# Attention loads in a written order: the next row tile's query stacks ahead of the latent keys and queries

## The chip, the cores and the metric

One core of one Trainium2 chip runs the whole program. The metric is device time in microseconds (us); three runs of the kernel before gave 1340.05, 1340.75 and 1341.09 us, median 1340.75.

## What is computed

A trunk of two equal layers on x of 1024 rows and 1024 columns, all in float32. A layer projects the normalised rows once, splits the columns among three attention groups, multiplies each group's output by a SiLU gate, and projects back. Cut to that:

```python
h = rms_norm(x, g_norm)
z = h @ w_in                      # 2656 columns, split among A, B, C and gates
oa = dense_gqa(qa, ka, va) * silu(ag)          # A: 6 heads, 2 key heads, all 1024 keys
ob = windowed_sink_gqa(qb, kb, vb) * silu(bg)  # B: 6 heads, 2 key heads, |i-j| <= 128
oc = mla(qc, kc, vc) * silu(cg)                # C: 4 heads from low-rank latents, all keys
x = x + concat(oa, ob, oc) @ w_out
```

A final RMSNorm closes the trunk.

## The kernel before

Each operand of a product is held as a high and a low part (`hi` rounded, `lo` the rest), so that a float32 product is two or three matmuls. Rows stand in 8 row tiles of 128 (`NS`).

A layer has these stages. The input projection makes rotated queries and keys of A and B (`pza`, `pzb`), the latents of C (`pzc`) and writes them to device memory: `d_q` (queries), `d_k` (keys of A and B), `d_kn` and `d_k3` (latent keys of C), `d_vc` (its values). Then `gate_units` computes the gates: 12 units here called g_m_hf (m the gate column block, hf the half of the rows), each 24 matmuls `pg`, one SiLU on ACT (L617) into a tile `g` that has two buffers, and one DMA of 256 KB to `d_gate`, issued by ACT itself. The last six, in this order, are g_3_0, g_4_0, g_5_0, g_3_1, g_4_1, g_5_1.

Then comes attention. Its loads are all issued by SyncE's queue (SP) through the helper `dma` (L97). First the tiles of the first row tile: `qsta` and `qstb` (query stacks of A and B, four DMAs of 96 KB each), `ka0`, `ka1` (high and low keys of A, two halves of 512 KB each), `kb0`, `kb1` (the same for B), a mask. Then latent values `vC` (1 MB), gates `gta`, `gtb`, `gtc`, latent keys `k1`, `k2`, `k3` (six DMAs, 2.25 MB), the latent queries `qc` of three row tiles (five DMAs each, 256 KB a tile), and the query stacks of the next row tile. The generator `units()` yields units of work: `UnitA` (scores `sa` of one A head, exp, transposes `ppa`, values `poa`), `UnitB` (scores `sb` of three B heads), `UnitC` (scores `sc`). For each row tile qt it makes two `Gqa` objects, whose constructor issues the stack loads; units of C come in from the second row tile on (`C_AT`).

The order of instructions on an engine isn't that of the code: a scheduler picks it, by priorities and a timeline of its own, except for instructions that `tc.keep_in_program_order` pins. What it picks is then fixed in the program.

Every DMA that SP or ACT issues also counts on one of eight completion counters, DMAHW0 to DMAHW7, called lanes below. SP's and ACT's DMAs take the lanes in turn, in the order in which the scheduler laid them down, and one that takes a lane is issued only when the lane's holder before it has landed. Waiting DMAs hold up all that stand behind them on their queue.

Of the kernel before, what the change touches and what calls it, by code (L numbers as in the profile page):

```python
# [45 lines left out]
def kernel(  # L46
# [25 lines left out]
    NS = S // P  # L72
# [6 lines left out]
    dram = ctx.enter_context(tc.tile_pool(name="dram", bufs=1, space=DRAM))  # L79

    queue_behind = [None]
    last_pow = [None]

    def after(ins, first):

        tc.add_manual_dep(
            ins,
            first.name,
            mybir.DependencyInfo(mybir.DependencyClass.NoSync, mybir.DependencyReason.DATA),
            reason="order",  # L90
        )
        return ins

    def dma(dst, src, eng=None):

        a, b = (t.bitcast(F32) if t.dtype == F32R else t for t in (dst, src))
        ins = (eng or nc.sync).dma_start(a, b)  # L97
        if queue_behind[0] is not None and eng is None:
            after(ins.ins, queue_behind[0])
        return ins.ins  # L100

    pinned = [False]
# [14 lines left out]

    ident = const.tile([P, P], F32, name="ident")
    dma(ident, c_ident)
    mhalf = const.tile([P, 8], F32, name="mhalf")  # L120
    nc.vector.memset(mhalf, -0.5)
# [19 lines left out]
    class Stage:  # L141
# [44 lines left out]
        def w_steps(self, ws, pieces, hi_eng=None, pool=None):  # L186
# [4 lines left out]
            for k0 in range(0, ND, kt):  # L191
                self.wcount += 1
                nm = f"{self.l}_{self.wcount}"
                st_ = self.p1.tile([P, 1024], F32, tag="wst", name=f"wst{nm}", bufs=2)
                if pool is None:
                    hi = self.p1.tile([P, 1024], F32R, tag="wh", name=f"wh{nm}", bufs=WBUFS)
                    lo = self.p1.tile([P, 1024], F32R, tag="wl", name=f"wl{nm}", bufs=WBUFS)
                else:
                    hi = pool.tile([P, kt * n], F32R, tag="wh", name=f"wh{nm}", bufs=ND // kt)
                    lo = pool.tile([P, kt * n], F32R, tag="wl", name=f"wl{nm}", bufs=ND // kt)  # L200
                st_ = st_.rearrange("p (k c) -> p k c", k=kt)
                hi, lo = (t.rearrange("p (k c) -> p k c", k=kt) for t in (hi, lo))
                o = 0
                for c, w in pieces:
                    self.last_w = dma(
                        st_[:, :, o : o + w],
                        w_in[self.l, k0 * P : (k0 + kt) * P, c : c + w].rearrange("(k p) c -> p k c", p=P),
                    )
                    o += w
                for k in range(0, kt, kt // 2):  # L210
                    ks = slice(k, k + kt // 2)
                    f, h, r = st_[:, ks, :n], hi[:, ks, :n], lo[:, ks, :n]
                    if hi_eng is A:
                        A.copy(h, f)
                    else:
                        G.tensor_scalar(h, f, 1.0, 0.0, ALU.mult, ALU.add)  # L216
                    V.tensor_tensor(out=r, in0=f, in1=h.bitcast(F32), op=ALU.subtract)
                his += [hi[:, k, :n] for k in range(kt)]
                los += [lo[:, k, :n] for k in range(kt)]
                yield  # L220
# [5 lines left out]
    for l in range(DEPTH):  # L226
# [18 lines left out]
        with stage.ph as ph:  # L245
# [32 lines left out]
            if l == 0:  # L278
# [6 lines left out]
                def load_x(st):  # L285
                    xts[st] = stage.px.tile([P, D], F32, tag="xt", name=f"xt{l}_{st}", bufs=XBUFS)
                    queue_behind[0] = dma(xts[st], x_src[st * P : (st + 1) * P, :])
# [61 lines left out]
            for i in range(2):  # L349
                gq = g_small[:, i * 64 : i * 64 + 64]  # L350
                ins = G.tensor_tensor(
                    out=tabs[:, :, 2 * i, :],
                    in0=rope_a[:, :, 0, :],
                    in1=gq.unsqueeze(1).to_broadcast([P, NS, 64]),
                    op=ALU.mult,
                )
                after(ins.ins, behind)
                gv = gq.rearrange("p (h a c) -> p h a c", h=2, a=2)
                for a in range(2):
                    for h in range(2):  # L360
                        o = h * 32 + a * 16
                        ins = G.tensor_tensor(
                            out=tabs[:, :, 2 * i + 1, o : o + 16],
                            in0=rope_a[:, :, 1, o : o + 16],
                            in1=gv[:, h, 1 - a, :].unsqueeze(1).to_broadcast([P, NS, 16]),
                            op=ALU.mult,
                        )
# [287 lines left out]
        with ExitStack() as ph:  # L655
# [113 lines left out]
            class Gqa:  # L769
# [29 lines left out]
                def finish(self):  # L799
                    G.tensor_tensor(out=self.o, in0=self.o, in1=self.gt, op=ALU.mult)  # L800
                    dma(d_o[:, self.m0 : self.m0 + 3, self.qt * P : (self.qt + 1) * P], self.o)

            def pipeline(units, spare):


# [12 lines left out]
                for u in itertools.chain(units, (None,)):  # L818
                    if callable(u):
                        queue += late  # L820
                        late = []
                        while queue:
                            fill()
                        u()
                        continue
                    if u is not None:
                        with tc.high_priority(SC_PRIO):
                            u.scores()
                    fill()
                    queue += late  # L830
                    late = []
                    if u is None:
                        for _ in range(SPARE):
                            next(spare, None)
                    if prev is not None:
                        t = prev.turn()
                        while True:
                            with tc.high_priority(T_PRIO):
                                if next(t, None) is None:
                                    break  # L840
                            fill()
                        late = [prev.values()]
                    prev = u
# [7 lines left out]


            if True:
                ks, start = {}, {}
                for g, m0 in (("a", 0), ("b", 3)):
                    start[g] = Gqa(g, 0, m0)
# [272 lines left out]
            def groups_c():  # L1129
                for hp in range(2):  # L1130
                    ks = KeysC(hp)
                    for q0 in range(0, NS, 3):
                        c = GroupC(ks, hp, q0)
                        if hp or q0:
                            c.gate()
                        else:

                            for it in (start["a"], start["b"], c):
                                it.gate()
                            yield None  # L1140
                        for par in range(2):
                            grp = {}
                            yield [UnitC(c, par, g, grp) for g in range(c.nq)]

            def units():

                cs = groups_c()
                next(cs)
                for qt in range(NS):
                    if qt == 0:  # L1150
                        a, b = start["a"], start["b"]
                    else:
                        a, b = Gqa("a", qt, 0), Gqa("b", qt, 3)
                        a.gate()
                        b.gate()
                    for kv in range(2):
                        grp = {}
                        for g in range(3):
                            yield UnitA(a, kv, g, grp)
                            if g == 1:  # L1160
                                yield UnitB(b, kv)
                        if 2 * qt + kv in C_AT:
                            yield from next(cs)
                first = True
                for us in cs:
                    for u in us:
                        yield u
                        if first:
                            yield ab_done
                            first = False  # L1170

            pipeline(units(), itertools.chain(*(out_part(*sc, 0, MW) for sc in ((0, 0), (0, 1), (1, 0), (1, 1)))))


# [128 lines left out]
```

## Time and profile before

| | |
|---|---|
| median of three runs | 1340.75 us |
| the profiled execution's own time | 1342.18 us |
| its span, first to last instruction | 1340.4 us |
| PE busy | 1301.9 us, 97% of the span |
| DVE, ACT, POOL busy | 67%, 54%, 39% |
| attention of the first layer begins (first `sa`) | 278.66 us |
| attention of the second layer begins | 936.60 us |

A group of rows below tells of one view. Times there are microseconds from the span's start. In a timeline a row is a run of equal instructions, "x4" says how many; "SPq" and "ACTq" are DMAs issued by that engine's queue, and their second column is the time that issuing took, not the transfer. Square brackets give the idle time of the engine before the row and what ended it. The granted clock (PEclk) is 1.00 at 2.4 GHz and 0.50 at 1.2 GHz.

### The profile page before, as it was taken

The page shows a single profiled execution, that of the slowest core. Times are in us where ns is not written, and L with a number is a line of the kernel's source. Part 1 is how long each engine was busy: PE and PEld are TensorE (multiplying, and loading weights), DVE is VectorE, ACT ScalarE, POOL GpSimd, SP SyncE. Part 2 cuts the span into 40 slices and gives each one's busy share as a digit, 9 for nine tenths or more (in the row PEclk, how much of TensorE's full clock was granted, in tenths as well). Part 3 has the DMA queues.
Part 4 walks back from the last instruction along what each step waited for, and adds up shares of the span by engine and source line. Part 5 has one row for each costly group of instructions (what it writes and reads, how often), then busy time and mean ns, then how long its engine had stood idle before and what let it go on. Part 6 is the DMA issues. An engine that isn't in the chain of part 4 may idle for free.

```text
span 1340.4 us, 21695 instructions
## 1 busy us (share of the span) xinstructions
PE 1301.9 (97%) x7320; PEld 1139.5 (85%) x7320; DVE 892.3 (67%) x2246; ACT 720.2 (54%) x1547; POOL 524.6 (39%) x602
## 2 busy tenths in 40 slices
PE   7999999989999999999999999999799999999997
PEld 7888998868989899888898889887698999998786
DVE  6685662057888988875537766600789899998543
ACT  4232341166888889842313324311688899897332
POOL 4330121025666676752023111300366766667100
PEclk8999999998999999999999999999899999999999
DMA  7234469353222432257323344783622225113443
GB/s 252 87 124 148 135 202 261 122 132 89 68 61 60 111 90 58 74 179 235 131 78 121 122 132 161 242 196 103 154 68 64 59 69 139 46 45 126 165 146 112
DMA packets 176878, 166.46 MB, mean 124 GB/s; under 512 B 22528, under 2 KB 149376, under 8 KB 176768
## 3 DMA queue, kind: packets, MB, share of 16 engines
q1 hardware_dynamic: 158016, 140.43, 36.5%
q10 hardware_dynamic: 18752, 24.65, 5.3%
q8 instruction: 58, 0.95, 0.3%
q14 instruction: 52, 0.43, 0.1%
HBM read 107.35 MB, written 57.67 MB: 123 GB/s over the span
## 4 chain that ended last, share of the span: by engine, by line
PE 82%; DVE 6%; DMA 5%; ACT 2%; issue 2%; SPq 2%; POOL 1%; POOLq 0%; DVEq 0%; ACTq 0%
PE pg L136 13%; PE pw L136 12%; PE pzb L114 7%; PE pza L114 7%; PE poa L136 6%; PE sc L136 5%; PE ppa L703 4%; PE pzc L136 4%; PE sa L136 4%; PE pzv L136 4%; PE ppc L703 3%; PE poc L136 3%; PE pob L136 2%; PE sb L136 2%; SPq L97 2%
## 5 line engine op out<-in xcount | busy, mean ns | idle before, releaser
L684 DVE CUSTOM_DVE_ANT_0 pa<-sa,zero 128x512 f32<-128x512 f32 x96 | 65.5, 682 | 136.6 <-PE sa L136 134.8
L711 POOL TENSOR_SCALAR ptha<-pfa 128x512 fp32r<-128x512 f32 x96 | 59.4, 621 | 206.7 <-ACT pfa L710 202.3
L712 POOL TENSOR_TENSOR ptla<-pfa,ptha 128x512 fp32r<-128x512 f32 x96 | 123.6, 1290 | 6.1
L136 PE MATMUL sa<-ka,qsta 128*128 128x512 f32 x384 | 121.3, 417 | 0.8 <-ACT g L617 0.7
L694 ACT ACTIVATE pa<-pa,nmxa 128x1024 f32<-128x1024 f32 x96 | 111.2, 1160 | 14.0 <-DVE nmxa L684 13.9
L136 PE MATMUL sc<-k,qc 128*128 128x512 f32 x384 | 111.5, 410 | 0.9 <-DVE nmxc L684 0.9
L703 PE MATMUL ppa<-ident,pa 128*128 128x128 f32 x768 | 106.3, 273 | 0.7 <-DVE ptlb L715 0.5
L703 PEld LDWEIGHTS ppa<-ident,pa 128*128 128x128 f32 x768 | 90.9, 141 | 14.8 <-DVE ptla L715 1.2
L136 PE MATMUL pw<-woh,oh 128*128 128x512 f32 x256 | 99.4, 394 | 2.1 <-ACT oh L1001 1.1
L136 PE MATMUL pw<-wol,oh 128*128 128x512 f32 x256 | 100.6, 394 | 0.8 <-DVE wol L1021 0.6
L136 PE MATMUL pg<-hTh,wh 128*128 128x512 f32 x256 | 100.3, 392 | 0.0
L136 PE MATMUL pg<-hTh,wl 128*128 128x512 f32 x256 | 100.2, 391 | 0.0
L136 PE MATMUL pg<-hTl,wh 128*128 128x512 f32 x256 | 100.1, 391 | 0.0
L136 PE MATMUL pw<-woh,ol 128*128 128x512 f32 x256 | 99.1, 393 | 0.3 <-DVE ol L1002 0.3
L216 POOL TENSOR_SCALAR wh<-wst 128x512 fp32r<-128x512 f32 (+1 forms) x64 | 39.6, 638 | 148.3 <-PE pzb L114 79.4
L617 ACT ACTIVATE g<-pg 128x512 f32<-128x512 f32 x32 | 19.1, 598 | 137.5 <-PE pg L136 90.5
L136 PE MATMUL poa<-ptha,vAB 128*128 128x384 f32 x256 | 89.4, 349 | 1.0 <-DVE ob L793 1.0
L136 PE MATMUL poa<-ptla,vAB 128*128 128x384 f32 x256 | 88.2, 344 | 0.0
L694 ACT ACTIVATE pc<-pc,nmxc 128x1024 f32<-128x1024 f32 x64 | 74.0, 1157 | 10.2 <-DVE nmxc L684 9.7
L136 PEld LDWEIGHTS sc<-k,qc 128*128 128x128 f32 x384 | 66.6, 189 | 10.7 <-DVE nmxc L684 2.0
L712 POOL TENSOR_TENSOR ptlc<-pfc,pthc 128x512 fp32r<-128x512 f32 x56 | 74.0, 1327 | 1.5
L684 DVE CUSTOM_DVE_ANT_0 pa<-sa,zero,nmxa 128x512 f32<-128x512 f32 x96 | 71.1, 743 | 4.5 <-PE sa L136 1.8
(217 smaller groups left out, 3817.3 us busy)
## 6 DMA issues: line engine op xcount, KB each, us to landing
wst<-in_w_in_dram SPq DMA_DIRECT2D x20, 512.0 KB, 3.6
d_gate<-g ACTq DMA_DIRECT2D x32, 256.0 KB, 2.4
wost<-in_w_out_dram SPq DMA_DIRECT2D x32, 256.0 KB, 2.9
wst<-in_w_in_dram SPq DMA_DIRECT2D x16, 384.0 KB, 4.4
qsta<-d_qa SPq DMA_DIRECT2D x64, 96.0 KB, 2.6
qstb<-d_qb SPq DMA_DIRECT2D x64, 96.0 KB, 2.6
k<-d_kn SPq DMA_DIRECT2D x12, 512.0 KB, 6.8
qc<-d_qc SPq DMA_DIRECT2D x96, 64.0 KB, 2.2
```

The source lines that it names most:

```text
L97: ins = (eng or nc.sync).dma_start(a, b)
L114: return lambda *a, **k: tc.keep_in_program_order(f(*a, **k))
L136: T.matmul(ps, lhsT=a, rhs=b, start=first and i == 0, stop=last and i == len(parts) - 1)
L216: G.tensor_scalar(h, f, 1.0, 0.0, ALU.mult, ALU.add)
L617: A.activation(g, ps, AF.Silu)
L684: V.tensor_tensor_reduce(p[:, c * 512 : (c + 1) * 512], ps, zero[:, 0:1].to_broadcast([P, 512]), -1.0, nmx[0][:, 0:1] if c else 3.0e38, AL ...
L694: A.activation(p, p, AF.Exp, scale=-1.0, bias=nmx[1][:, 0:1], accum_out=sm)
L703: T.transpose(pt[:, (j - q0) * P : (j - q0 + 1) * P], p[:, j * P : (j + 1) * P], ident)
L711: G.tensor_scalar(hi, f, 1.0, 0.0, ALU.mult, ALU.add)
L712: G.tensor_tensor(out=lo, in0=f, in1=hi.bitcast(F32), op=ALU.subtract)
```

## The change

Loads through `dma` on SP are pinned to the order of the code from the start of the attention stage until the first latent loads and gates have been issued (`in_order`). In `units()` the query stacks of the second row tile are created before the first gates, the latent keys and the latent queries; those of later row tiles are created half a row tile earlier in the code, at `kv == 1` of the row tile before. The gates of the first row tile's A and B are loaded ahead of the latent keys, C's behind the latent queries.

```diff
     def dma(dst, src, eng=None):
         ...
         if queue_behind[0] is not None and eng is None:
             after(ins.ins, queue_behind[0])
+        if in_order[0] and eng is None:
+            tc.keep_in_program_order(ins)
         return ins.ins
...
             if True:
+                in_order[0] = True
                 ks, start = {}, {}
...
                         if hp or q0:
                             c.gate()
                         else:
-
-                            for it in (start["a"], start["b"], c):
-                                it.gate()
+                            c.gate()
                             yield None
...
             def units():
 
+                a, b = start["a"], start["b"]
+                ahead = Gqa("a", 1, 0), Gqa("b", 1, 3)
+                a.gate()
+                b.gate()
                 cs = groups_c()
                 next(cs)
+                in_order[0] = False
                 for qt in range(NS):
-                    if qt == 0:
-                        a, b = start["a"], start["b"]
-                    else:
-                        a, b = Gqa("a", qt, 0), Gqa("b", qt, 3)
+                    if qt:
+                        a, b = ahead
                         a.gate()
                         b.gate()
                     for kv in range(2):
+                        if kv and 0 < qt < NS - 1:
+                            ahead = Gqa("a", qt + 1, 0), Gqa("b", qt + 1, 3)
```

What it does to the program can be seen at three places of the first layer; the second layer reads alike. In the rows the line comes first, then the operation, what it writes and reads (tile names carry layer, row tile and a serial number), its shape, and in brackets the counters that it waits for: a lane DMAHWn, or an engine's counter.

On SP, the first loads of attention, before:

```order
L97 DMA ka0_0_2789<-d_ka0_81 64x2x1024 [waits DMAHW7_49]
L97 DMA ka0_0_2789<-d_ka0_81 64x2x1024 [waits DMAHW0_49]
L97 DMA ka1_0_2792<-d_ka0_81 64x2x1024 [waits DMAHW1_49]
L97 DMA ka1_0_2792<-d_ka0_81 64x2x1024 [waits DMAHW2_49]
L97 DMA qstb0_0_2795<-d_qb0_79 64x3x128 [waits DMAHW3_49]
L97 DMA qstb0_0_2795<-d_qb0_79 64x3x128 [waits DMAHW4_49]
L97 DMA qstb0_0_2795<-d_qb0_79 64x3x128 [waits DMAHW5_49]
L97 DMA qstb0_0_2795<-d_qb0_79 64x3x128 [waits DMAHW7_49]
L97 DMA kb0_0_2802<-d_kb0_82 64x2x1024 [waits DMAHW0_49,PE_49]
L97 DMA kb0_0_2802<-d_kb0_82 64x2x1024 [waits DMAHW1_49]
L97 DMA kb1_0_2805<-d_kb0_82 64x2x1024 [waits DMAHW6_49,DMAHW2_49,Activation_49]
L97 DMA kb1_0_2805<-d_kb0_82 64x2x1024 [waits DMAHW3_49]
```

and after:

```order
L98 DMA ka0_0_2789<-d_ka0_81 64x2x1024 [waits DMAHW3_49]
L98 DMA ka0_0_2789<-d_ka0_81 64x2x1024 [waits DMAHW4_49]
L98 DMA ka1_0_2792<-d_ka0_81 64x2x1024 [waits DMAHW5_49]
L98 DMA ka1_0_2792<-d_ka0_81 64x2x1024 [waits DMAHW6_49]
L98 DMA qstb0_0_2795<-d_qb0_79 64x3x128 [waits DMAHW7_49]
L98 DMA qstb0_0_2795<-d_qb0_79 64x3x128 [waits DMAHW0_49]
L98 DMA qstb0_0_2795<-d_qb0_79 64x3x128 [waits DMAHW1_49]
L98 DMA qstb0_0_2795<-d_qb0_79 64x3x128 [waits DMAHW2_49]
L98 DMA kb0_0_2802<-d_kb0_82 64x2x1024 [waits DMAHW3_49,PE_49]
L98 DMA kb0_0_2802<-d_kb0_82 64x2x1024 [waits DMAHW4_49]
L98 DMA kb1_0_2805<-d_kb0_82 64x2x1024 [waits DMAHW5_49,Activation_49]
L98 DMA kb1_0_2805<-d_kb0_82 64x2x1024 [waits DMAHW6_49]
```

The loads stand in the same order in both lists, but hold and wait for other lanes.

On ACT, the last six gate units, before. An ACTIVATE here waits for the lane of the store two units ahead, since `g` has two buffers, and so shows which lane that store holds:

```order
L97 DMA d_gate0_77<-g0_3_0_2609 128x512 [waits DMAHW3_49,Activation_49]
L617 ACTIVATE g0_4_0_2637<-pg0_4_0_2612 128x512 [waits DMAHW2_49,PE_49]
L97 DMA d_gate0_77<-g0_4_0_2637 128x512 [waits DMAHW4_49,Activation_49]
L617 ACTIVATE g0_5_0_2665<-pg0_5_0_2640 128x512 [waits DMAHW3_49,PE_49]
L97 DMA d_gate0_77<-g0_5_0_2665 128x512 [waits DMAHW5_49,Activation_49]
L617 ACTIVATE g0_3_1_2693<-pg0_3_1_2668 128x512 [waits DMAHW4_49,PE_49]
L97 DMA d_gate0_77<-g0_3_1_2693 128x512 [waits Activation_49]
L617 ACTIVATE g0_4_1_2721<-pg0_4_1_2696 128x512 [waits DMAHW5_49,PE_49]
L97 DMA d_gate0_77<-g0_4_1_2721 128x512 [waits Activation_49]
L617 ACTIVATE g0_5_1_2749<-pg0_5_1_2724 128x512 [waits DMAHW6_49,PE_49]
L97 DMA d_gate0_77<-g0_5_1_2749 128x512 [waits Activation_49]
```

and after:

```order
L98 DMA d_gate0_77<-g0_3_0_2609 128x512 [waits Activation_49]
L620 ACTIVATE g0_4_0_2637<-pg0_4_0_2612 128x512 [waits DMAHW0_49,PE_49]
L98 DMA d_gate0_77<-g0_4_0_2637 128x512 [waits Activation_49]
L620 ACTIVATE g0_5_0_2665<-pg0_5_0_2640 128x512 [waits DMAHW1_49,PE_49]
L98 DMA d_gate0_77<-g0_5_0_2665 128x512 [waits Activation_49]
L620 ACTIVATE g0_3_1_2693<-pg0_3_1_2668 128x512 [waits DMAHW2_49,PE_49]
L98 DMA d_gate0_77<-g0_3_1_2693 128x512 [waits Activation_49]
L620 ACTIVATE g0_4_1_2721<-pg0_4_1_2696 128x512 [waits DMAHW3_49,PE_49]
L98 DMA d_gate0_77<-g0_4_1_2721 128x512 [waits Activation_49]
L620 ACTIVATE g0_5_1_2749<-pg0_5_1_2724 128x512 [waits DMAHW4_49,PE_49]
L98 DMA d_gate0_77<-g0_5_1_2749 128x512 [waits Activation_49]
```

Before, the stores of g_3_0, g_4_0 and g_5_0 take lanes 3, 4 and 5 behind loads that hold them. After, the stores have their lanes first (g_3_0 lane 1, g_4_0 lane 2, g_5_0 lane 3, g_3_1 lane 4, g_4_1 lane 5), the scheduler having laid them down ahead of the loads: the wait values of the built program name the store of g_5_0 for the first half of `ka0`, g_3_1 for its second, g_4_1 for the first half of `ka1`, and g_5_1 (lane 0) for the second quarter of `qstb`. The last loads of `qsta`, ahead of these rows, wait for g_3_0 and g_4_0.

On PE, the first B scores, of row tile 0, before:

```order
L136 MATMUL sa0_0_0_1_1_2869<-ka0_0_2789,qsta0_0_2782 128x512
L136 MATMUL sa0_0_0_1_1_2869<-ka1_0_2792,qsta0_0_2782 128x512
L136 MATMUL sb0_0_0_0_2896<-kb0_0_2802,qstb0_0_2795 128x256
L136 MATMUL sb0_0_0_0_2896<-kb1_0_2805,qstb0_0_2795 128x256
L136 MATMUL sb0_0_0_1_2900<-kb0_0_2802,qstb0_0_2795 128x256
L136 MATMUL sb0_0_0_1_2900<-kb1_0_2805,qstb0_0_2795 128x256
L136 MATMUL sb0_0_0_2_2904<-kb0_0_2802,qstb0_0_2795 128x256
L136 MATMUL sb0_0_0_2_2904<-kb1_0_2805,qstb0_0_2795 128x256
L136 MATMUL sa0_0_0_2_0_2937<-ka0_0_2789,qsta0_0_2782 128x512
```

and after:

```order
L139 MATMUL sa0_0_0_1_1_2883<-ka0_0_2789,qsta0_0_2782 128x512
L139 MATMUL sa0_0_0_1_1_2883<-ka1_0_2792,qsta0_0_2782 128x512
L139 MATMUL sb0_0_0_0_2910<-kb0_0_2802,qstb0_0_2795 128x256
L139 MATMUL sb0_0_0_1_2914<-kb0_0_2802,qstb0_0_2795 128x256
L139 MATMUL sb0_0_0_2_2918<-kb0_0_2802,qstb0_0_2795 128x256
L706 MATMUL ppa0_0_0_0_0_2892<-ident_63,pa0_0_0_0_2866 128x128
```

After, the 16 transposes of the first two A heads stand between the two halves of the B scores; eight `sa` matmuls stand ahead of all this in both. Further on, the first three `sc` matmuls stand ahead of the three `prb` and 16 `poa` matmuls that they follow before. On SP the loads behind the mask run, after, in the written order: `qsta` and `qstb` of row tile 1, `gta`, `gtb`, `k1`, `k2`, `k3`, `vC`, then the `qc` of three row tiles.

## Rows read from the trace of the kernel before

**Rows 1.** Waits of PE: line waited for, us in total, times, longest.
```profile
PE sb L136 <- DMA qstb<-d_qb: 12.8, 4, 6.5
```

**Rows 2.** Timeline of PE: start, us, engine, line, operation [idle before].
```profile
278.66 2.15 PE L136 MATMUL sa<-ka,qsta 128*128 128x512 f32 x8
...
284.81 1.04 PE L703 MATMUL ppa<-ident,pa 128*128 128x128 f32 x8
...
303.45 0.98 PE L136 MATMUL sb<-kb,qstb 128*128 128x384 f32 x2 [6.50 <-DMA qstb<-d_qb]
...
960.64 0.98 PE L136 MATMUL sb<-kb,qstb 128*128 128x384 f32 x2 [5.62 <-DMA qstb<-d_qb]
```

**Rows 3.** Stretches: busy us of PE, PEld, DVE, ACT, POOL; granted clock; DMA share, GB/s.
```profile
284.20:296.90 12.70, 12.13 (x74) 9.45 (x72) 12.15 (x36) 12.67 (x33) 7.96 (x9) 1.00 0.98 201
296.90:303.40 6.50, 0.04 (x1) 0.00 (x0) 2.30 (x8) 3.36 (x8) 2.02 (x3) 0.61 0.32 90
303.40:308.60 5.20, 4.91 (x15) 4.18 (x16) 3.78 (x13) 0.36 (x1) 0.28 (x1) 0.50 0.69 190
...
960.60:967.40 6.80, 6.30 (x20) 5.54 (x21) 4.47 (x13) 2.40 (x8) 1.48 (x2) 0.50 0.63 181
```

**Rows 4.** Timeline of SP's queue at the first layer's attention loads.
```profile
212.48 2.54 SPq L97 DMA_DIRECT2D ka<-d_ka  x4
...
265.25 0.37 SPq L97 DMA_DIRECT2D gtb<-d_gate  x1
...
277.48 2.48 SPq L97 DMA_DIRECT2D qsta<-d_qa  x4
...
281.90 2.19 SPq L97 DMA_DIRECT2D k<-d_kn  x3
...
300.97 1.82 SPq L97 DMA_DIRECT2D qstb<-d_qb  x3
```

**Rows 5.** Timeline of ACT's queue: the stores of g_5_0, g_3_1 and g_4_1.
```profile
263.16 0.33 ACTq L97 DMA_DIRECT2D d_gate<-g  x1
...
268.60 0.33 ACTq L97 DMA_DIRECT2D d_gate<-g  x1
...
274.04 0.33 ACTq L97 DMA_DIRECT2D d_gate<-g  x1
```

**Rows 6.** The chain that ended last, in order of time: start, us, what.
```profile
279.48 2.34 DMA d_gate<-g
281.90 0.58 SPq L97
...
285.42 10.77 DMA k<-d_k
...
307.56 0.64 PE prb L763 x3
308.20 3.05 PE poa L136 x16
...
311.72 0.70 PE sc L136 x3
...
324.24 0.93 PE sa L136 x4
...
328.43 0.35 PE sb L136 x2
```

**Rows 7.** Tile ka, 205 to 235 us: issues (ns each, first and last start), us to landing.
```profile
L97 SPq DMA_DIRECT2D ka<-d_ka x4: 585/601/607, 212.5 to 214.4; - x4
...
DMA to landing us min/median/max: 4.7/7.5/10.2
```

**Rows 8.** Tile vC, 240 to 300 us: its one load, then us to landing.
```profile
L97 SPq DMA_DIRECT2D vC<-d_vc x1: 556/556/556, 244.8 to 244.8; - x1
...
DMA to landing us min/median/max: 6.5/6.5/6.5
```

More of the change, by code (lines that the diff above doesn't have):

```diff
@@ L81 @@
     queue_behind = [None]
+    in_order = [False]
     last_pow = [None]
```

## The prediction

> **What bounds the kernel now.** PE does: it is busy for 1301.9 of the 1340.4 us span, so only what PE waits for, or runs slowly through, can move the time. I read PE's waits first: the longest entry is B's first scores of row tile 1, `sb`, waiting for the query stack `qstb`, 12.8 us in four pieces [rows 1]. PE's timeline places it: 6.50 us up to 303.45 in the first layer, 5.62 us up to 960.64 in the second [rows 2]. Then the stretches, for the clock: it falls to 0.50 (1.2 GHz) during the stall, and stays there for 5.20 us of the work after it, in the second layer for 6.80 us [rows 3]. PE is busy there for 4.91 and 6.30 us, which at 2.4 GHz would be half, so 2.45 and 3.15 us are lost behind each stall. The two stalls are thus worth 6.50 + 2.45 + 5.62 + 3.15 = 17.7 us. SP's queue shows the cause: the last three quarters of `qstb` are issued at 300.97, behind six latent key loads and 15 query loads that begin at 281.90 [rows 4].
>
> The chain of waits shows a second thing, which I read as the heart of this case. The load at 281.90 is released by a gate store, issued by ACT at 279.48 and landing 2.34 us later [rows 6]: a load of latent keys, held by the lane that a store of gates had before it. In the kernel before this costs little, because the first tiles' loads (`ka` at 212.48, [rows 4]) hold their lanes ahead of the late stores.
>
> **What the change moves.** It removes no instruction and adds none on PE, DVE, ACT or POOL. It moves the stacks of row tile 1 ahead of the latent loads, which would end the stall above; that edit alone is worth up to 17.7 us. It moves the latent values from 244.8 [rows 8], where nobody waited, to behind the latent keys. And it moves the first tiles' loads behind the gate stores in the lanes. This last is what the order of the program shows and the diff doesn't: `ka`, `qstb` and `kb` now wait for lanes that the stores of g_5_0, g_3_1, g_4_1 and g_5_1 hold. I follow the first layer, on the clock of the trace before, as nothing ahead of 278.66 depends on these loads and PE is busy with gates until then.
>
> First the loads. The g_5_0 store is issued at 263.16 [rows 5]; `gtb`, which needs it, was issued at 265.25 [rows 4], 2.1 us later. With that landing time the halves of `ka0` go out at 265.3 and 270.7, those of `ka1` at 276.1 and 276.7 (one issue is 0.60 us), a quarter of `qstb` at 277.3. The next quarter needs the store of g_5_1, so it goes at 281.9, as the key load did before. Two quarters more, and the four halves of `kb` go out from 283.7 on. What a half takes to land is in the loads of `ka`: 4.7 us for the first, and the last, issued 1.9 us behind, lands 7.4 us after it, so 2.5 us for each more [rows 7]. `ka1` has landed by 276.1 + 4.7 + 2.5 = 283.3; `kb` lands at 288.4, 290.9, 293.4 and 295.9.
>
> Now PE. It begins `sa` at 278.66, and stops at the first product with `ka1` until 283.3. The B scores with `kb0` wait until 290.9, and those with `kb1` until 295.9, with 16 transposes between them. At 296.4 PE has done 8 `sa`, 6 `sb` and 16 transposes. Before, the second eight transposes begin at 284.81 and are done by about 285.6 [rows 2], and six more `sa` are done, 1.4 us at 0.93 us for four [rows 6]: the same work was done at 284.2. So PE is 12.2 us late, at the least clock 1.00.
>
> From there to the first C score PE has 12.7 us of the work up to the old stall, at a busy share of 12.13 in 12.70 us [rows 3], then six `sb` and four `sa` and two transposes, 2.2 us by the chain's rows (0.35 for two `sb`, 0.93 for four `sa`, [rows 6]): it would be there at 311.3. ACT, at 12.67 of 12.70 us [rows 3], has caught up during the stall and doesn't hold it back.
>
> But the C loads are late too. Behind `kb` come sink and mask (until 287.3) and the stacks of row tile 1, eight loads that again go by lanes: the third waits for the first half of `kb0` (288.4), the fifth and sixth for the halves of `kb1` (293.4, 295.9); the last is out at 297.1 and in place before PE wants it, so the old stall is gone. `gta` and `gtb` follow, and the six key loads begin at 298.3. Before, they began at 281.90 and the last landed at 285.42 + 10.77 = 296.2 [rows 6], 14.3 us; so 312.6. Then `vC`, 1 MB, 6.5 us alone [rows 8], of which some 2.2 are the dead time that `ka` shows too (4.7 less 2.5): 4.3 to 5.0 us, I take 4.5, so 317.1. The first tile of latent queries, 256 KB, lands 1.3 us behind: 318.4. The first C score waits for it.
>
> Before, that score began at 311.72, behind three `prb` and 16 `poa` (0.64 + 3.05 us, [rows 6]) which now stand after it: on equal work 308.0. The layer is 10.4 us late there. The old 308.0 has the slow clock's 2.45 us in it; the new stall of 7 us will bring it again behind 318.4, at 0 to 2.45 us that aren't in the sum. I take half, 1.2. So 11.6 us a layer, 23.2 in all, since the second layer's lists and waits are the same. The rest of attention is PE-bound with small stalls; a shuffled order there I price at nothing, within 2 us either way.
>
> **Sum.** The profiled execution took 1342.18 us, span and 1.8 us around it; plus 23.2 is 1365.4. The median of the runs is 1.4 below the profiled one: 1364.
>
> **The rivals.** *The query loads overtake the latent values.* The sum lets a 256 KB load land behind the 1 MB in front of it. The halves of `ka` landed in the order of issue, 4.7 to 10.2 us [rows 7], which speaks for that. The Trainium skill's page "DMA: Bandwidth & Descriptors", section "Queues, rings and completion order", says that completion is not first in, first out for an issuing engine; by it the small loads could land early, while the trace shows loads of one shape alone. If they do, the first C score is held by the keys, 312.6 + 1.3 = 313.9, 5.9 us late and 1.2 for the clock: 14.2 in all, 1355.
>
> *Only the first stall stays.* If keys and values land as PE comes to them, the first C score is at 311.3, 3.3 us late, and 2.45 or less for the slow clock: 4.6 a layer, 1350. For it: behind 296.90 the DMA share before is only 0.32 and 0.69 [rows 3], so there is room if loads go out sooner than I reckon. Against: 3.5 MB of keys, values and queries stand between 298.3 and the first C score, and such loads ran at 201 GB/s with a share of 0.98 [rows 3].
>
> *It does what it says, and is faster.* This needs the first keys in place when PE asks for them; the point from which it decides is the last half of `kb1` landing by some 282, so the first half of `ka0` being issued by some 250 instead of 265.3. That is so if the lanes' waits are met early, the stores being small. Then the stacks of row tile 1 go out from 277.48 as before, both old stalls go, and the C keys, issued from 283.7, land at 298.0, values at 302.5, queries at 303.8, 4.2 us ahead of the old 308.0. With nothing else 1342.2 - 8.4 - 1.4 = 1332; with the C loads hidden too 1323. Against it: each of these waits is of the kind that held `gtb` until 265.25 and the keys until 281.90.
>
> **How the numbers follow.** The forecast has 0.60, with its own spread 1358 to 1372; the overtaking queries 0.13, only the first stall 0.11, the gain 0.07; 0.04 for a near balance within 0.2%, and 0.05 for more than 1372 (a longer slow clock behind three stalls). From 1347 to 1372 holds the first three, less some of their edges: 0.8. A measurement can tell about 0.2%, 2.7 us. Faster 0.07, same 0.04, slower 0.89. Predicted: 1364 us.
>
> **What the profile of the changed kernel would show.** If right: `ka` issued between 265 and 277 and `kb` from about 284, no longer from 212; PE waiting for `ka` and `kb` at the start of attention, by 4 and some 10 us in each layer, and for `qc` or `k` at the first `sc`, by about 7; the wait of `sb` for `qstb` gone; the granted clock at 0.50 in two places of each layer's start. If wrong: `kb` landed ahead of 282 makes it a gain; no wait at the first `sc` makes it the smaller loss; a first C score released by the keys, not the queries, is the overtaking.

## The result, and the profile after

The kernel after takes 1371.7 us (four runs, 1370.6 to 1372.7) against 1340.4 us (four runs, 1340.05 to 1341.09): a ratio of 1.0233, 95% interval 1.0215 to 1.025. It is slower, by 31.3 us; the forecast was 1364 us, in a range from 1347 to 1372.

The four largest waits of PE in the kernel after (line, what ended the wait, us in total, times, longest us), which answer [rows 1]:

```profile
PE sc L139 <- DMA qc<-d_qc: 12.8, 2, 7.0
PE sb L139 <- DMA kb<-d_kb: 8.9, 3, 7.6
PE sb L139 <- issue: 7.7, 1, 7.7
PE sa L139 <- DMA ka<-d_ka: 6.8, 2, 3.8
```

The wait for `qstb` is gone, and three others stand in its place. The row "issue" is the second layer's wait for `kb`, for which the profile names no releaser: PE's timeline puts it at the same instruction as the first layer's. Of that timeline, first layer and then second (idle time before the row in brackets), to be held against [rows 2]:

```profile
275.52 0.84 PE L139 MATMUL sa<-ka,qsta 128*128 128x512 f32 x3
280.13 2.78 PE L139 MATMUL sa<-ka,qsta 128*128 128x512 f32 x5 [3.77 <-DMA ka<-d_ka]
290.54 0.98 PE L139 MATMUL sb<-kb,qstb 128*128 128x256 f32 x3 [7.63 <-DMA kb<-d_kb]
...
295.30 0.59 PE L139 MATMUL sb<-kb,qstb 128*128 128x256 f32 x3 [0.98 <-DMA kb<-d_kb]
...
317.68 1.62 PE L139 MATMUL sc<-k,qc 128*128 128x512 f32 x3 [5.81 <-DMA qc<-d_qc]
...
964.68 0.98 PE L139 MATMUL sb<-kb,qstb 128*128 128x256 f32 x3 [7.74 <-issue]
...
993.00 1.62 PE L139 MATMUL sc<-k,qc 128*128 128x512 f32 x3 [6.99 <-DMA qc<-d_qc]
```

Attention begins 3.14 us sooner here (275.52 against 278.66 us). The change has no part in that: between the first `pza` matmul and the first `sa` lie 231.45 us after and 231.46 us before; the difference is older than that, where the profiled execution of before had a stretch of lower clock (its page gives PEclk 8 in the first of 40 slices) that the other didn't have. It is no matter of the kernel either: from one profile of this study to another the first `sa` begins between 275.5 and 279.0 us, always 231.45 us behind the first `pza`. So I compare from the first `sa` on.

SP's queue at the first layer's loads, which answers [rows 4]:

```profile
262.07 12.08 SPq L98 DMA_DIRECT2D ka<-d_ka  x4
274.19 8.53 SPq L98 DMA_DIRECT2D qstb<-d_qb  x4
282.82 2.56 SPq L98 DMA_DIRECT2D kb<-d_kb  x4
...
292.71 4.28 SPq L98 DMA_DIRECT2D qstb<-d_qb  x4
...
298.26 1.89 SPq L98 DMA_DIRECT2D k<-d_kn  x3
...
302.32 0.59 SPq L98 DMA_DIRECT2D vC<-d_vc  x1
302.96 18.35 SPq L98 DMA_DIRECT2D qc<-d_qc  x15
```

`ka` goes out 50 us later than before (212.48, [rows 4]) and its four DMAs take 12.08 us to issue, not 2.54, since three of them stand at a lane of a gate store: the stores of g_5_0, g_3_1 and g_4_1 landed at 262.05, 267.46 and 272.90 us, and the first three halves of `ka` were issued at 262.07, 267.48 and 272.92. The chain of waits names what holds whom, where [rows 6] had one such step. These are its DMAs in order of time (start, us from issue to landing):

```profile
270.90 2.00 DMA d_gate<-g
...
273.54 6.46 DMA ka<-d_ka
...
284.77 10.39 DMA kb<-d_kb
...
299.55 9.74 DMA k<-d_kn
...
309.30 8.24 DMA qc<-d_qc
```

A gate store releases `ka`; the last half of `kb` holds a lane that a stack of row tile 1 wants; a half of the latent keys holds one that a load of the first latent queries wants. So the chain goes over from ACT's stores to PE's first C score.

Where the time went, by stretches. Columns are the stretch, its length, busy us of PE, PEld, DVE, ACT, POOL with their instructions, granted clock, DMA share, GB/s. Each layer's attention is cut at the same number of PE's instructions (129 from the first `sa`, then the rest up to the first `pw`). Before:

```profile
278.66:311.30 32.64, 24.99 (x129) 20.04 (x128) 24.45 (x77) 23.41 (x56) 11.48 (x13) 0.84 0.70 168
311.30:573.42 262.12, 259.41 (x1648) 235.48 (x1647) 229.63 (x620) 224.08 (x477) 179.36 (x199) 1.00 0.28 77
936.60:969.40 32.80, 25.79 (x129) 20.77 (x130) 25.59 (x79) 23.39 (x57) 11.48 (x13) 0.84 0.69 167
969.40:1230.62 261.22, 259.07 (x1647) 235.46 (x1646) 230.30 (x617) 224.87 (x477) 179.44 (x199) 1.00 0.27 75
```

And after:

```profile
275.52:322.50 46.98, 27.20 (x129) 21.34 (x128) 22.74 (x79) 21.90 (x50) 9.98 (x11) 0.78 0.86 193
322.50:586.45 263.95, 261.00 (x1648) 235.25 (x1647) 227.88 (x620) 225.66 (x484) 181.12 (x201) 1.00 0.30 82
950.20:998.10 47.90, 28.28 (x129) 22.20 (x129) 22.44 (x80) 21.35 (x49) 9.98 (x11) 0.75 0.84 186
998.10:1261.49 263.39, 260.40 (x1647) 235.13 (x1647) 227.32 (x618) 225.08 (x483) 180.68 (x201) 1.00 0.30 82
```

The first 129 instructions take 14.3 and 15.1 us longer, the other 1,648 and 1,647 only 1.8 and 2.2 us: 33.4 us in all, less the 3.1 us of the start, against 30.5 us between the two spans. So the loss sits in the first 47 us of each layer's attention, and 12.1 of its 14.3 us in the first layer are idle time (46.98 - 27.20 = 19.8 us, before 32.64 - 24.99 = 7.7 us); for the rest PE is busy longer, at a lower clock (0.78, before 0.84). The two sets of 129 differ a little: three `sc` of the kernel after (0.70 us) stand where before has three `prb` (0.33 us), so that some 0.4 us a layer could as well be put to the second stretch. The clock at the two stalls of the first layer (columns as above):

```profile
279.90:293.50 13.60, 5.74 (x19) 4.33 (x20) 2.74 (x8) 2.83 (x5) 0.00 (x0) 0.50 0.81 182
...
313.90:320.80 6.90, 3.12 (x9) 2.86 (x10) 0.81 (x4) 0.00 (x0) 0.00 (x0) 0.51 0.55 132
```

It is down, at its 1.2 GHz level, in two places, as in [rows 3] it was in one.

### The profile page after: what moved, and what is told of

Read it like the earlier page. It is cut to its first block, busy times and chain, and to the rows that moved or that the text cites. A ratio compares the mean times of both kernels' runs of the same rounds, so it can differ in the third digit from the quotient of the medians.

```text
span 1370.9 us, 21682 instructions
## 1 busy us (share of the span) xinstructions
PE 1306.5 (95%) x7320; PEld 1138.3 (83%) x7320; DVE 882.3 (64%) x2246; ACT 718.9 (52%) x1547; POOL 524.6 (38%) x602
## 4 chain that ended last, share of the span: by engine, by line
PE 73%; DMA 10%; DVE 6%; ACT 4%; issue 3%; POOL 2%; SPq 1%; POOLq 0%; ACTq 0%; DVEq 0%
PE pg L139 12%; PE pw L139 7%; PE pzb L117 6%; PE pza L117 6%; PE poa L139 6%; PE sc L139 5%; PE pzc L139 4%; PE ppa L706 4%; PE sa L139 4%; PE pzv L139 3%; PE ppc L706 3%; PE poc L139 2%; DMA ol<-d_o 2%; PE pob L139 2%; DMA kb<-d_kb 2%
## 5 line engine op out<-in xcount | busy, mean ns | idle before, releaser
L139 PE MATMUL sc<-k,qc 128*128 128x512 f32 x384 | 114.5, 415 | 13.7 <-DMA qc<-d_qc 12.8
L697 ACT ACTIVATE pa<-pa,nmxa 128x1024 f32<-128x1024 f32 x96 | 111.2, 1159 | 23.7 <-DVE nmxa L687 23.5
L706 PEld LDWEIGHTS ppa<-ident,pa 128*128 128x128 f32 x768 | 93.0, 144 | 13.6 <-PE sa L139 1.9
L139 PEld LDWEIGHTS sa<-ka,qsta 128*128 128x128 f32 x384 | 65.0, 192 | 22.1 <-issue 7.6
L718 DVE TENSOR_TENSOR ptla<-ppa,ptha 128x512 fp32r<-128x512 f32 x96 | 64.8, 682 | 22.8 <-ACT ptha L717 21.8
```

Of the source, the lines that this page charges most:

```text
L139: T.matmul(ps, lhsT=a, rhs=b, start=first and i == 0, stop=last and i == len(parts) - 1)
L697: A.activation(p, p, AF.Exp, scale=-1.0, bias=nmx[1][:, 0:1], accum_out=sm)
L706: T.transpose(pt[:, (j - q0) * P : (j - q0 + 1) * P], p[:, j * P : (j + 1) * P], ident)
L718: V.tensor_sub(lo, ptv, hi.bitcast(F32))
```

## Experiments

Three theories stood at the start. **Lanes**: the mark (the pinning of SP's loads to the order of the code) puts the first loads behind the gate stores in the eight lanes. **Order**: the new order of the queue, stacks ahead and values late, costs the time by itself. **Overtaking**: the queries don't wait for the values. The ratios below are to the kernel before, which was run beside each of them on the same chip (1342.6 to 1343.7 us there, 1340.4 us in the first row).

| kernel | median us | ratio | 95% interval |
|---|---|---|---|
| the change | 1371.7 | 1.0233 | 1.0215 to 1.025 |
| the change without its mark | 1338.4 | 0.9964 | 0.9951 to 0.9978 |
| before, with the mark alone | 1392.5 | 1.0358 | 1.0322 to 1.0393 |
| the change, gate stores on GpSimd | 1336.4 | 0.9949 | 0.993 to 0.9968 |
| the change, values last | 1364.4 | 1.0168 | 1.0139 to 1.0196 |
| without mark, values last | 1328.9 | 0.9898 | 0.988 to 0.9917 |
| without mark, first stacks only | 1348.4 | 1.0039 | 1.0025 to 1.0054 |
| before, gate stores on GpSimd | 1342.6 | 1.0003 | 0.9994 to 1.0012 |
| without mark, values first | 1329.3 | 0.9905 | 0.9888 to 0.9922 |
| the change, stacks before low keys | 1378.0 | 1.026 | 1.0245 to 1.0275 |
| the change, stores on GpSimd, values last | 1331.6 | 0.9923 | 0.9911 to 0.9935 |

### The change without its mark

```diff
             if True:
-                in_order[0] = True
                 ks, start = {}, {}
```

> The kernel after without its one line that marks the loads to keep the written order; the stacks of row tile 1 stand ahead of the latent keys, and the latent values behind them, as in the kernel after. Lanes (my theory): the first tiles' loads stand ahead of the gate stores again, so `ka`, `qstb` and `kb` are issued before 255 us and PE waits for none of them; the stall for the stacks of row tile 1 is gone too (their loads go out from about 277); at the first C score there is at most a small wait, for values and queries. Time 1323 to 1335 us. Rival (the new order of the queue, stacks ahead and values late, costs the time by itself, whatever the first tiles' loads do): 1355 us or more, with a wait at the first C score of 6 us in each layer.

It is faster than before, 0.9964. SP's queue of this kernel, and the one wait for a load that PE has left in its first layer:

```profile
212.63 3.51 SPq L98 DMA_DIRECT2D ka<-d_ka  x4
...
277.21 2.48 SPq L98 DMA_DIRECT2D qsta<-d_qa  x4
...
287.63 0.59 SPq L98 DMA_DIRECT2D vC<-d_vc  x1
```

```profile
304.12 1.62 PE L139 MATMUL sc<-k,qc 128*128 128x512 f32 x3 [4.71 <-DMA qc<-d_qc]
```

The first loads are back at 212 us, the waits for `ka`, `kb` and `qstb` are all gone, and the rest of the queue stands in the order of the kernel after. So that order doesn't cost the 31 us; the mark does, on the first tiles' loads. The time is above the 1323 to 1335 us I expected: a wait for `qc` of 4.7 and 2.5 us is left.

### The mark alone

```diff
 (kernel before, with `in_order` and the line in `dma` that reads it)
...
             if True:
+                in_order[0] = True
                 ks, start = {}, {}
...
                 next(cs)
+                in_order[0] = False
                 for qt in range(NS):
```

> The kernel before with the mark on its attention loads and nothing else of the change: the stacks of row tile 1 stay behind the latent loads. Lanes: the first tiles' loads go behind the gate stores as in the kernel after (`ka` issued from 262 to 274 us, `kb` from about 283), so PE waits for them 11 to 12 us in each layer; the C loads follow some 5 us sooner than in the kernel after, since no stacks stand ahead, so the wait at the first C score is smaller, 0 to 4 us; the stacks of row tile 1 are last, and PE still waits for them. In all 1360 to 1385 us, I take 1372. Rival (the mark only fixes what the scheduler did anyway, and the loss comes from the stacks ahead): 1340 us, no wait for `ka` or `kb`.

It is the slowest of all, 1.0358. Its four largest waits of PE:

```profile
PE sa L139 <- DMA qsta<-d_qa: 16.5, 2, 9.1
PE sb L139 <- DMA kb<-d_kb: 8.8, 3, 8.1
PE sb L139 <- issue: 7.6, 1, 7.6
PE sa L139 <- DMA ka<-d_ka: 7.0, 2, 3.9
```

`ka` and `kb` stall as in the kernel after, so the mark does that without the stacks ahead. Two things I had too small: the stacks of row tile 1, now behind 15 query loads (issued at 320.87 us), stop PE for 9.1 and 7.4 us at `qsta`, the A half of them, and the first layer's output stage (`pw`) takes 117.7 us, before 106.8. That second one is no matter of lanes at the start of attention, and comes back below.

### The gate stores on another queue

```diff
-    dma(d_gate[:, m0 + m, hf * 512 : (hf + 1) * 512], g, nc.scalar)
+    dma(d_gate[:, m0 + m, hf * 512 : (hf + 1) * 512], g, nc.gpsimd)
```

> The kernel after with the gate stores issued by GpSimd's queue instead of ScalarE's, nothing else; the order of SP's queue is that of the kernel after. Lanes: SP's loads no longer follow a gate store in a lane, so `ka`, `qstb` and `kb` land before 275 us, the waits for them are gone, and the C loads go out from about 285; 1323 to 1340 us. Rival 1 (SP's order by itself holds the loads, or the bytes in flight do, not the stores): 1372 us with the same waits. Rival 2 (the stores' issue on GpSimd delays its own work, and so the gates): waits of PE during the gates that the kernel after doesn't have.

This leaves the mark and the order of SP's queue as they are, and takes the stores out of the lanes (in the trace they count on counters that no DMA of SP or ACT uses). SP's queue and, of its waits, the only one for a load of attention that is over 1 us:

```profile
211.03 2.59 SPq L98 DMA_DIRECT2D ka<-d_ka  x4
...
218.69 7.29 SPq L98 DMA_DIRECT2D kb<-d_kb  x4
```

```profile
PE sc L139 <- DMA qc<-d_qc: 1.3, 1, 1.3
```

0.9949: the loss is gone with the mark still there. The same edit in the kernel before tells whether the stores alone do it:

> The kernel before with its gate stores issued by GpSimd's queue, nothing else of the change. It tells whether the gain of the third experiment came from these stores alone. Lanes: the kernel before doesn't wait for a gate store at `ka` or `kb`, and its stall for `qstb` stands behind the latent loads, not the stores, so little changes: 1335 to 1343 us, with the wait for `qstb` there (4 to 7 us in each layer). Rival (the stores in the lanes cost the kernel before as well): the wait for `qstb` gone or under 2 us a layer, and 1325 to 1333 us.

Nothing: 1.0003, with the wait of `sb` at 13.6 us in two pieces (put down to "issue", as above). So the stores cost time only where loads stand behind them in the lanes, and the mark costs only where stores stand ahead. Together with the kernel without the mark this shows the lanes from both sides.

### The values behind the queries

```diff
                         c = GroupC(ks, hp, q0)
+                        if q0 == 0:
+                            dma(ks.v, d_vc[:, :, 2 * hp : 2 * hp + 2, :])
```

(and the same load taken out of `KeysC`, where it stood behind the keys.)

> The kernel after with the 1 MB load of latent values moved behind the first C group's query loads, for both halves of the heads; nothing else. If the queries land behind the values, as the forecast had it: the first C score comes 4 to 5 us sooner in each layer, the wait for `qc` falls from 12.8 us in two pieces to about 4, and the time to 1362 us (1360 to 1365). If the queries overtook the values, or the keys decide: 1372 us as the kernel after, with the wait put down to `k`. If PE only meets the next late load instead (the values at the first product with them): a part of the wait goes over to `vC`, and 1365 to 1372 us.

1.0168, with the wait for `qc` down from 12.8 to 4.8 us and none for `vC`:

```profile
PE sc L139 <- DMA qc<-d_qc: 4.8, 2, 2.7
```

The first C score comes 39.6 and 37.8 us after the first `sa`, in the kernel after 42.2 and 42.8: 2.6 and 5.0 us, where I had put 4.5 a layer. (In the first layer of this profile the key loads began 0.7 us later after the first `sa` than in the kernel after, which is in the 2.6.) The queries had waited for the values, then; overtaking falls. The same edit without the mark, and the values put first instead:

> The first experiment's kernel (change without the mark) with the latent values moved behind the first C group's queries as well. There PE waited 7.2 us for `qc` (4.7 and 2.5), and the clock fell behind the larger of the two. Lanes and the order of landing: this wait goes to 0 to 2 us, and the time 6 to 9 us below that kernel, about 0.990 of before. Rival (queries wait for the lanes of the keys, wherever the values stand): the wait stays at 5 us or more, about 0.996 of before.

```diff
                 dma(mask, c_mask)
+                v0 = cv.tile([P, NS, 2, P], F32R, tag="vC", name=f"vC{l}_0")
+                dma(v0, d_vc[:, :, 0:2, :])
```

(and the first half's load taken out of `KeysC`.)

> The first experiment's kernel with the first half's latent values loaded ahead of everything of the C group, right behind the first tiles' loads, as the kernel before has them. They are in place long before attention begins, so the queries stand behind the keys alone: the wait at the first C score 0 to 2 us, the time as that of the kernel with values last or 1 to 2 us below it, about 0.990 of before. If the early 1 MB holds back loads that PE needs: new waits for `ka` or `kb`, and no gain over the first experiment.

0.9898 and 0.9905, both with no wait for a load over 0.3 us at the first C score. These two are the best of the study, some 13 us under the kernel before. The stretches of the first of them, cut as above:

```profile
277.38:302.60 25.22, 23.83 (x129) 18.06 (x128) 23.68 (x79) 23.56 (x57) 11.53 (x13) 1.00 0.78 181
302.60:566.37 263.77, 261.14 (x1648) 235.43 (x1647) 229.18 (x619) 223.96 (x477) 179.67 (x199) 1.00 0.32 87
931.57:957.00 25.43, 23.91 (x129) 18.21 (x130) 23.79 (x79) 23.03 (x56) 11.53 (x13) 1.00 0.75 179
957.00:1220.66 263.66, 261.06 (x1648) 235.35 (x1647) 228.87 (x618) 223.29 (x476) 179.00 (x199) 1.00 0.31 86
```

With all its loads in time the first stretch takes 25.2 us, 7.4 under before, and the rest still 1.7 and 2.4 us over before. That remainder, then, has nothing to do with the stalls: the clock is 1.00, PE is busy for 99% of it, and the same number of instructions in the new order keeps it busy for 261.1 us, before for 259.4.

### Only the first stacks ahead

```diff
 (without the mark)
                     if qt:
+                        if qt > 1:
+                            ahead = Gqa("a", qt, 0), Gqa("b", qt, 3)
                         a, b = ahead
...
-                        if kv and 0 < qt < NS - 1:
-                            ahead = Gqa("a", qt + 1, 0), Gqa("b", qt + 1, 3)
```

> The first experiment's kernel with the stacks of row tile 1 ahead as there, but those of the later row tiles made where the kernel before makes them. In the two kernels with the new order a layer's attention comes 1.5 to 2.3 us further behind the kernel before, counted at equal numbers of PE's instructions, from the 128th to the last, with no wait to be named. If making the later stacks half a row tile earlier does that: this drift is gone and the time is 3 to 4 us below the first experiment's. If the stacks don't matter (the order of PE's work at the first C scores does it): the same time and the same drift as there.

The second stretch of each layer, and then the first layer's output stage of this kernel:

```profile
307.00:568.91 261.91, 259.48 (x1645) 234.49 (x1643) 228.91 (x617) 222.49 (x476) 178.94 (x199) 1.00 0.30 82
...
974.10:1236.50 262.40, 259.53 (x1644) 234.40 (x1642) 229.45 (x618) 222.64 (x476) 178.73 (x199) 1.00 0.30 83
568.91:688.20 119.29, 110.02 (x527) 90.52 (x526) 64.01 (x99) 35.60 (x66) 26.81 (x32) 0.96 0.46 145
```

The drift goes from 1.7 and 2.6 us (the same kernel with the later stacks early) to -0.2 and 1.2. This kernel puts four transposes `ppc`, some 0.4 us, behind its first `pw`, so on equal work it is 0.2 and 1.6: by one profile of each, rather over half of the drift comes from making the later stacks half a row tile earlier. The time I expected from that was wrong by its sign all the same, 1.0039: the output stage takes 119.3 us instead of 108.0. On SP's queue the store of C's output there stands behind 13 weight loads (`wost`, 24 us to issue); in the kernel before, behind 9. PE waits 8.2 us there for `oh`, which is made from that output. The kernel with the mark alone, where the later stacks are also made at the old place, lost 11 us in the same stage, with 11 weight loads ahead of that store. That it is the store's place I have only read, not tried.

### The last gate store

The step of the forecast on which the later ones hung is the landing of the last gate store, g_5_1. Of the tile `g` in the kernel after, this store and its landing (us, minimum, median, maximum):

```profile
L98 ACTq DMA_DIRECT2D d_gate<-g x1: 326/326/326, 276.3 to 276.3; - x1
...
DMA to landing us min/median/max: 4.5/4.5/4.5
```

In [rows 6] it took 2.34 us. Beside it, in the kernel after, the 1 MB of `ka1` is in flight (issued at 272.92 and 273.54, landing 6.46 us after the second). The experiment swaps `ka1` with the stacks of B:

```diff
-                for g, m0 in (("a", 0), ("b", 3)):
-                    start[g] = Gqa(g, 0, m0)
-                    for i in range(2):
-                        t = pk.tile([P, 2, S], F32R, name=f"k{g}{i}_{l}")
...
+                start["a"] = Gqa("a", 0, 0)
+                keys("a", 0)
+                start["b"] = Gqa("b", 0, 3)
+                keys("a", 1)
+                keys("b", 0)
+                keys("b", 1)
```

> The kernel after with one swap in the written order: the first row tile's stacks of B stand ahead of the low keys of A, `ka1`, which are 1 MB. It tests why the last gate store (g_5_1), which holds a quarter of `qstb` and with it all that stands behind, took 4.5 us to land in the kernel after instead of the 2.3 of the kernel before. If the 1 MB of `ka1` in flight beside it did that: here `ka1` is behind that store, and it lands in 2.0 to 2.8 us; the quarter goes out about 2 us sooner after the store, but `ka1` 3 us later than it did, so PE waits 6 to 8 us at the first product with it; `kb1`, bound by 3 MB in a row, lands within 2 us of where it did. Time 1368 to 1378 us. If something else at the end of the gates holds the store: 4 to 5 us again.

```profile
L98 ACTq DMA_DIRECT2D d_gate<-g x1: 327/327/327, 278.9 to 278.9; - x1
...
DMA to landing us min/median/max: 2.0/2.0/2.0
```

2.0 us: the store was slow because of `ka1`. PE's wait for `ka1` became 10.2 and 9.6 us, more than the 6 to 8 expected, and the time 1.026. The trace of before has such a row too, an earlier gate store with the 1 MB of `vC` in flight (issued at 244.8, [rows 8]); of tile `g`, 246 to 248 us:

```profile
L97 ACTq DMA_DIRECT2D d_gate<-g x1: 326/326/326, 246.8 to 246.8; - x1
...
DMA to landing us min/median/max: 5.7/5.7/5.7
```

### The mark where no store stands ahead

The change with the stores on GpSimd's queue and the values last, two edits shown above in one kernel:

> The third experiment's kernel (the change with its mark, gate stores on GpSimd's queue) with the latent values behind the first C group's queries. There PE waited 1.3 us for `qc` and the clock fell in the first layer for a short time. If the mark costs nothing once no gate store stands ahead of the loads in the lanes: as the two best so far, 0.988 to 0.993 of before, with no wait for any load over 1 us in attention. If the mark costs by itself: 0.995 or more.

0.9923, and PE waits for no load of attention there. Its interval just overlaps that of the best kernel without the mark (0.988 to 0.9917): a cost of the mark itself isn't clearly seen, the two ratios being 0.25% apart.

## Why the prediction was right, and where it was short

**The mechanism held.** Put on the clock of before (plus 3.14 us), the halves of `ka0` went out at 265.2 and 270.6 us (forecast 265.3 and 270.7), those of `ka1` at 276.1 and 276.7 (276.1 and 276.7), the first quarter of `qstb` at 277.3 (277.3). PE stood 3.8 us for `ka1` (forecast 4), then for both parts of `kb`, then at the first C score, and the wait for `qstb` was gone. Removing the mark, or the stores from the lanes, removes the stalls.

**The step that was mis-sized is the landing of the store of g_5_1.** I took 2.34 us from a row of before, where only loads of 96 KB were in flight beside the store; in the changed kernel my own sum had the 1 MB of `ka1` in flight at that moment. It took 4.5 us (4.6 in the second layer). The row to take stood in the same trace: 5.7 us beside the 1 MB of `vC`. Everything behind inherits the 2.2 us: the next quarter of `qstb` went out at 284.0 instead of 281.9, `kb` from 286.0 instead of 283.7, its last half landed at 298.3 instead of 295.9, the first C score began at 320.8 instead of 318.4. So the layer was 12.8 us late there, not 10.4. That the 2.2 us arrive there so nearly unchanged is in part luck: the key loads began at 301.4 us (forecast 298.3) and the last landed at 316.2 (312.6), over 1 us more than was inherited, and the values then needed 3.5 us behind the keys, not 4.5.

**The clock behind the second stall** I put at 1.2 us. From 12.8 us late at the first C score to 14.3 at the 129th instruction, it is 1.5; in the second layer 13.7 to 15.1, 1.4; the 0.4 us of other work among the 129 is in these. At the first stall PE runs at 1.2 GHz too, but waits for `kb` right after, so that little is lost by it.

**The shuffled order** I priced at nothing, within 2 us. It costs 1.8 and 2.2 us a layer, at the edge of that, and also where no load is waited for; rather over half of it is the later stacks. Why PE is busy longer in that order stays open.

**The sum.** Forecast 10.4 + 1.2 + 0 = 11.6 us a layer; measured 12.8 + 1.5 + 1.8 = 16.1 and 13.7 + 1.4 + 2.2 = 17.3. Twice 11.6 is 23.2, and 33.4 was lost (30.5 us between the two spans, since attention began 3.1 us sooner). That 1371.7 us still lies within the 1347 to 1372 of the forecast is luck: it does so by 0.3 us, and two of the four runs took 1372.6 and 1372.7.

**The gain was over-sized.** I put the old stalls and their clock at 17.7 us. In the kernel with all loads in time the first stretches are 7.4 us shorter each, 14.8 in all. The stalls themselves were 12.1 [rows 2]; what is left for the clock behind them is some 2.7, not 5.6. Why it is less I haven't tested; DVE and ACT are busy for 23.7 and 23.6 of the 25.2 us of that kernel's first stretch, so they may hold PE there where the clock no longer does. The 17.7 entered only the rival of the gain, not the sum of the forecast.

**The rivals.** That the queries overtake the values: the five loads of the first query tile landed 7.2 to 13.9 us after they were issued, all behind the values (302.32 + 14.2 = 316.5 us); even the sink, a small load issued right behind `kb`, took this long:

```profile
DMA to landing us min/median/max: 10.0/10.0/10.0
```

that is, until 295.4 us, just behind the last half of `kb`. The forecast held that the trace of before shows loads of one shape alone. That was misread: the first query load there, issued at 286.06 us behind the keys, took 10.4 us, and the sink, again behind `kb` (its issue, KB, us to landing), no less:

```profile
sink<-in_b_sink_dram SPq DMA_DIRECT2D x1, 3.0 KB, 12.0
```

The Trainium skill's page "DMA: Bandwidth & Descriptors", section "Queues, rings and completion order", says that completion isn't first in, first out for an issuing engine. On SP's queue it was here: in none of the twelve traces did one of that queue's 716 DMAs land ahead of one issued before it. That only the first stall stays: no, the C loads came 2.4 us later than the forecast, not sooner. That it does what it says: only without the mark, or with the stores elsewhere, and then 1336 to 1338 us, not the 1332 or 1323 I gave it, since the values stood ahead of the queries.

## What to carry to other kernels

When loads are pinned to a written order, read which lane each of them takes and who held it before: a load can be made to wait for a store that it has nothing to do with, and here loads issued 50 us early cost nothing, while the same loads at their "right" place stalled the bound engine. Take the landing time of a transfer from a row in which as much else is in flight as will be in the changed kernel. And put what is needed last, here the latent values, last on the queue or long ahead of it; this alone was worth some 0.65% of the time here, with the mark and without it.

## What the hardware showed unexpectedly

A 256 KB store issued by ACT landed in 2.0 us when alone, and in 4.5 us (beside `ka1`) and 5.7 us (beside `vC`) with 1 MB of SP's loads in flight. And the sink, six numbers to each of 128 partitions (3 KB), issued on SP's queue right behind the 2 MB of `kb`, took 10.0 us: on that queue, in all of these traces, a small load landed no sooner for being small.
